# Token sums three chunks later in the attention's first product, a tile of its own for one copy, and another place in memory for the splits of V

## The chip, the core and the metric

The kernel runs on one core of a Trainium2 chip. A core has a matrix engine (TensorE, PE in the profile, with its weight loads as PEld), a vector engine (DVE), a scalar engine (ACT), GpSimd (POOL) and a queue engine (SP); PE writes its results to PSUM, and the other engines move them to the on-chip memory (SBUF). The metric is the device time of one execution in microseconds, as the median of several runs.

## What is computed

A decoder trunk of two residual layers over 512 tokens of 1024 numbers. Layer 0 mixes tokens by causal pooling, layer 1 by dilated window attention with 16 heads; each is followed by a gated feed-forward part (FFN) of width 2816, and one last norm ends the trunk.

```python
def reference(x, ...):
    for i in range(DEPTH):                       # DEPTH = 2
        h = rmsnorm(x, norm_mix[i])
        y = pool_mixer(h, ...) if i % 2 == 0 else attn_mixer(h, ...)
        x = x + y
        h = rmsnorm(x, norm_ffn[i])
        x = x + swiglu(h, ffn_w_gate[i], ffn_w_up[i], ffn_w_down[i])
    return rmsnorm(x, norm_final)

def swiglu(h, w_gate, w_up, w_down):
    return (silu(h @ w_gate) * (h @ w_up)) @ w_down
```

## The kernel before

**Layout and precision.** Everything is transposed: x lies as 8 chunks of 128 features by 512 tokens. A product in full precision is made of three PE products (`mm3`, lines 194 to 196): every operand is split into a rounded part "hi" (a cast on ACT, line 118 for weights, 326 for others) and a rest "lo" (a subtraction on DVE, lines 119 and 327), and hi x hi, hi x lo and lo x hi are added up in PSUM.

**Weights.** One list holds all weight blocks in the order of use. `weights(i)` loads some blocks ahead into `wraw` or `vraw` tiles and splits some ahead into `whi`/`wlo` or `vhi`/`vlo`. There are two kinds, "w" (three split buffers) and "v" (two); "v" blocks exist in the FFN only, where some blocks are sums of two blocks (line 114, and an adding DMA on POOL, line 98).

**FFN.** Pairs of output blocks are made with seven products in the place of eight (`seven`, line 563 is its only matmul, 128x256 each). `quad(n)` makes the gate and up blocks from h; `down(b, half)` multiplies the result u by the down weights. The seven products i = 0 to 6 go to the PSUM tiles p, r, p, q, p, r, p. Products 1, 2 and 5 take a "v" block as weights, the other four a "w" block. A product of a quad has 24 matmuls, one of a down 18. The two layers have 18 quads and 12 such downs in all. The moving operands of a quad are quarters of `h_hi`/`h_lo` (products 0, 1, 3 and 5) and sums of quarters in tiles `t_hi`/`t_lo` (products 2, 4 and 6); those of a down are `u_hi`/`u_lo`.

**What follows a product.** `done(i, ...)` moves each sum out of PSUM. In a quad, product 0 is copied by ACT from p into `ct[:, 0, 0]` (line 581), and product 2 cannot start before that, since it writes p again. `ct` is also what `first_half` and `second_half` of the previous pair read when they split u into `u_hi` (ACT) and `u_lo` (DVE, line 327). So line 581 has to wait until DVE has read the old `ct`:

```python
nc.scalar.copy(ct[:, 0, 0], p)                      # quad, product 0 (line 581)
split(hi[:, 0:2, :], lo[:, 0:2, :], lst[:, 0:2, :])  # the pair before: reads ct[:, 0, 0]
```

A down has three `keep` tiles of its own for such copies (line 620).

**Places in memory.** Pools lie one behind the other in SBUF. Nearly all tiles are multiples of 256 bytes long per partition, and the tiles `h_hi`, `h_lo`, `whi`, `wlo`, `vhi`, `vlo`, `u_hi` and `u_lo` all start 160 bytes past a multiple of 256. `gap4`, a tile of 32 numbers (128 bytes) that nothing uses, moves the six `t` tiles behind it to 32 bytes past a multiple of 256; `gap5`, another such tile, moves what follows back.

**Norm.** The norm factor of a token needs the sum of squares over all features. ACT squares each finished chunk of x (line 246), POOL adds the first six into one tile (line 250), and the last two are kept apart where the FFN of layer 0 ends (`Norm(2)`). `InverseRms.columns` adds up these three tiles per token with 128x1 matmuls (line 269: four token blocks by three tiles), and DVE and ACT make the factor of them (lines 300, 256 to 261) and put it on diagonals (lines 280, 282); `rows` spreads it over the partitions with four matmuls (line 289) and a copy (line 307). The products that need no factor yet go on meanwhile: a hook says before which chunk of a product the two steps stand in PE's order. The first product of the attention (q of heads 0 and 1) begins while the last chunks of x are still being made:

```python
pq = project([j_qk[2 * t]], h_hi, h_lo, KS, None, None if t else {4: inv_rms.columns})
pk = project([j_qk[2 * t + 1]], h_hi, h_lo, KS, None, {2: inv_rms.rows})   # t == 0
```

**Order.** PE's order is the order in which the code is written. On the other engines a scheduler sets the order; each engine then runs its own list strictly in that order.

## Time and profile before

| | |
|---|---|
| runs: median of 3 (lowest to highest) | 1048.31 us (1047.85 to 1048.71) |
| the profiled execution's own time | 1047.12 us |
| its span, first to last instruction | 1045.4 us |
| PE busy | 1018.0 us, 97% of the span |
| DVE busy | 802.6 us, 77% |
| ACT busy | 517.5 us, 50% |
| POOL busy | 189.4 us, 18% |
| mean granted clock of PE | 0.99 of full speed |

Between the profiled execution's time and its span lie 1.7 us. PE is busy nearly all the time, so only three things can change the total: what PE waits for, how fast its matmuls follow each other, and the clock that it is granted. A matmul's duration in the profile overlaps the next one's, so the pace is read from the starts.

### The profile page before, as it was taken

How to read it: one execution, taken by the hardware profiler on the slowest of the kernel's cores; microseconds unless marked ns; L12 is line 12 of the kernel's file. 1: busy time of each engine (PE TensorE's matmuls, PEld its weight loads, DVE VectorE, ACT ScalarE, POOL GpSimd, SP SyncE). 2: the span in 40 equal slices, each digit the busy share in tenths (PEclk: the TensorE clock that was granted, in tenths of full speed). 3: DMA queues.
4: the chain of work that ended last, by engine and by line, in shares of the span. 5: the costliest groups of instructions: out<-in, count | busy, mean ns of one | idle time of the engine just before them, and what ended most of it. 6: DMA issues, size and time to landing. Idle time of an engine off the chain costs nothing.

```text
span 1045.4 us, 17409 instructions
## 1 busy us (share of the span) xinstructions
PE 1018.0 (97%) x6986; PEld 939.5 (90%) x6986; DVE 802.6 (77%) x1100; ACT 517.5 (50%) x797; POOL 189.4 (18%) x163
## 2 busy tenths in 40 slices
PE   8979999999999999999999999999999999999996
PEld 6758888999999999978777899888999999999996
DVE  6794489888888888675988645559989789788844
ACT  6243446554655555452344533454665555455544
POOL 1742300111111111022233210210011110101003
PEclk9989999999999999998999999999999999999998
DMA  7132445669669767432212233524558867966702
GB/s 265 62 101 93 139 120 137 141 175 230 153 162 240 177 137 195 133 113 81 81 41 66 64 114 102 140 81 103 140 140 220 205 148 162 241 157 156 183 35 81
DMA packets 75201, 144.19 MB, mean 138 GB/s; under 512 B 6384, under 2 KB 30576, under 8 KB 75120
## 3 DMA queue, kind: packets, MB, share of 16 engines
q1 hardware_dynamic: 56992, 113.33, 34.5%
q0 software_dynamic: 16320, 28.32, 16.9%
q10 hardware_dynamic: 1808, 1.43, 0.4%
q8 instruction: 54, 0.88, 0.4%
q14 instruction: 27, 0.22, 0.1%
HBM read 140.96 MB, written 2.10 MB: 137 GB/s over the span
## 4 chain that ended last, share of the span: by engine, by line
PE 82%; DVE 10%; issue 3%; DMA 2%; ACT 2%; POOL 1%; SPq 0%; ACTq 0%; DVEq 0%; POOLq 0%
PE p L563 28%; PE r L563 14%; PE mm L194 8%; PE mm L195 8%; PE mm L196 8%; PE mm L563 7%; DVE wlo L119 2%; DMA vraw<-w 1%; PE mm L269 1%; PE mm L1005 1%; PE mm L1004 1%; PE mm L1006 1%; PE early L194 1%; PE tp L871 1%; PE early L195 1%
## 5 line engine op out<-in xcount | busy, mean ns | idle before, releaser
L118 ACT CAST whi<-wraw 128x1024 fp32r<-128x1024 f32 (+4 forms) x201 | 194.2, 967 | 260.8 <-PE p L563 101.8
L119 DVE TENSOR_TENSOR wlo<-wraw,whi 128x1024 fp32r<-128x1024 f32 (+4 forms) x201 | 231.3, 1151 | 40.0 <-ACT whi L118 38.9
L119 DVE TENSOR_TENSOR vlo<-vraw,vhi 128x1024 fp32r<-128x1024 f32 (+1 forms) x90 | 100.3, 1116 | 42.0 <-ACT vhi L118 40.6
L118 ACT CAST vhi<-vraw 128x1024 fp32r<-128x1024 f32 (+1 forms) x90 | 86.8, 965 | 83.6 <-PE r L563 55.6
L196 PE MATMUL mm<-h_hi,wlo 128*128 128x512 f32 x312 | 122.6, 393 | 2.8 <-DVE wlo L119 2.8
L194 PE MATMUL mm<-h_hi,whi 128*128 128x512 f32 x312 | 124.8, 400 | 0.0
L195 PE MATMUL mm<-h_lo,whi 128*128 128x512 f32 x312 | 122.5, 393 | 0.0
L563 PE MATMUL r<-h_hi,vlo 128*128 128x256 f32 x288 | 81.5, 283 | 0.0
L563 PE MATMUL r<-h_lo,vhi 128*128 128x256 f32 x288 | 81.5, 283 | 0.0
L563 PE MATMUL r<-h_hi,vhi 128*128 128x256 f32 x288 | 81.4, 283 | 0.0
L563 PE MATMUL p<-t_hi,whi 128*128 128x256 f32 x288 | 81.2, 282 | 0.0
L563 PE MATMUL p<-t_lo,whi 128*128 128x256 f32 x288 | 81.1, 282 | 0.0
L563 PE MATMUL p<-t_hi,wlo 128*128 128x256 f32 x288 | 81.0, 281 | 0.0
L196 PEld LDWEIGHTS mm<-h_hi,wlo 128*128 128x128 f32 x312 | 59.1, 189 | 16.0 <-DVE wlo L119 3.2
L194 PEld LDWEIGHTS mm<-h_hi,whi 128*128 128x128 f32 x312 | 59.2, 190 | 14.4 <-issue 1.7
L195 PEld LDWEIGHTS mm<-h_lo,whi 128*128 128x128 f32 x312 | 59.2, 190 | 11.8
L114 DVE TENSOR_TENSOR vraw<-vraw,wraw 128x1024 f32<-128x1024 f32 (+1 forms) x60 | 66.7, 1112 | 0.6
L563 PE MATMUL p<-u_hi,whi 128*128 128x256 f32 x216 | 61.2, 283 | 0.1
L563 PE MATMUL p<-u_hi,wlo 128*128 128x256 f32 x216 | 61.1, 283 | 0.0
L563 PE MATMUL p<-u_lo,whi 128*128 128x256 f32 x216 | 61.1, 283 | 0.0
L98 POOL DMA_DIRECT2D wraw<-w x18 | 21.8, 1209 | 216.1 <-DVE ct L513 47.9
L250 POOL TENSOR_TENSOR ssq<-ssq,sq 128x512 f32<-128x512 f32 x20 | 32.2, 1608 | 141.2 <-issue 76.4
(278 smaller groups left out, 3012.7 us busy)
## 6 DMA issues: line engine op xcount, KB each, us to landing
wraw<-w SPq DMA_DIRECT2D x131, 512.0 KB, 3.8
wraw<-w_down SPq DMA_DIRECT2D x48, 384.0 KB, 3.4
vraw<-w SPq DMA_DIRECT2D x18, 512.0 KB, 6.1
vraw<-w POOLq DMA_DIRECT2D x18, 512.0 KB, 7.4
wraw<-w POOLq DMA_DIRECT2D x18, 512.0 KB, 7.4
vraw<-w_down SPq DMA_DIRECT2D x12, 384.0 KB, 4.0
vraw<-w_down POOLq DMA_DIRECT2D x12, 384.0 KB, 5.8
wraw<-w_down POOLq DMA_DIRECT2D x12, 384.0 KB, 7.3
```

Of the source, the lines that this page charges most:

```text
L98: nc.gpsimd.dma_start(dst, more, accum_op=ALU.add)
L114: nc.vector.tensor_add(raw[:, :n], raw[:, :n], raws[item["plus"]][:, :n])
L118: nc.scalar.copy(hi[:, :n], raw[:, :n])
L119: nc.vector.tensor_sub(lo[:, :n], raw[:, :n], hi[:, :n].bitcast(F32))
L194: nc.tensor.matmul(ps, lhsT=whi, rhs=xhi, start=first, stop=False)
L195: nc.tensor.matmul(ps, lhsT=whi, rhs=xlo, start=False, stop=False)
L196: nc.tensor.matmul(ps, lhsT=wlo, rhs=xhi, start=False, stop=last)
L250: nc.gpsimd.tensor_add(self.ssq, self.ssq, sq)
L269: nc.tensor.matmul(cols[:, i : i + 1], lhsT=sq[:, b * P : (b + 1) * P], rhs=ones[:, :1], start=j == 0, stop=j == len(parts) - 1,)
L563: nc.tensor.matmul(ps[:, g, :], lhsT=w[:, g, c, :], rhs=xx, start=i in (0, 1, 3) and g + c + k == 0, stop=c == n - 1 and k == 2, skip_grou ...
L871: nc.tensor.transpose(tp[:, j, :], todo[i + j], ident)
L1004: nc.tensor.matmul(o, lhsT=xh, rhs=whi[:, kk, :], start=kc == 0, stop=False)
```

## The change

It has four edits.

- In the attention's first product the token sums stand before chunk 7 in place of chunk 4, and the spreading of the factor before chunk 4 of the next product in place of chunk 2.
- In a quad, the copy of product 0 goes into `keep[0]`, and the sum after product 3 reads it from there. The three `keep` tiles are made once for the FFN and shared by quads and downs.
- `gap5` moves to a pool of its own between the pool of V and that of the early u tiles. Behind `gap4` without it, `ct`, `keep`, `vraw`, `vhi` and `vlo` now start 32 bytes past a multiple of 256; the u tiles stay where they were.
- Of the `t` tiles the pair for product 2 (the one of a "t" sum with a "v" block) lies ahead of `gap4`, at 160 bytes; the other two pairs lie behind it, at 32 bytes as before.

```diff
@@ ffn
             pools["v"] = open_pool("ffv", 2)
+            open_pool("ffg", 1).tile([P, 32], F32, name="gap5")
             early_u = open_pool("ffa", 2)
...
+            t_tile = lambda i, part: fp.tile([P, 4, 256], F32R, name=f"t_{part}{i}")
+            t2 = [t_tile(2, part) for part in ("hi", "lo")]
             fp.tile([P, 32], F32, name="gap4")
-            T_hi = [block(h_hi, 0, 1)] + [fp.tile([P, 4, 256], F32R, name=f"t_hi{i}") for i in range(1, 4)]
-            T_lo = [block(h_lo, 0, 1)] + [fp.tile([P, 4, 256], F32R, name=f"t_lo{i}") for i in range(1, 4)]
-            fp.tile([P, 32], F32, name="gap5")
+            t3, t4 = ([t_tile(i, part) for part in ("hi", "lo")] for i in (3, 4))
+            T_hi, T_lo = ([block(h, 0, 1), t2[i], t3[i], t4[i]] for i, h in enumerate((h_hi, h_lo)))
...
             lst = ct.rearrange("p m n g c -> p (m n g) c")
+            keep = [fp.tile([P, 2, 256], F32, name=f"keep{i}") for i in range(3)]
@@ quad, done
                     if i == 0:
-                        nc.scalar.copy(ct[:, 0, 0], p)
+                        nc.scalar.copy(keep[0], p)
...
                     elif i == 3:
-                        nc.vector.tensor_add(ct[:, 0, 0], q, ct[:, 0, 0])
+                        nc.vector.tensor_add(ct[:, 0, 0], q, keep[0])
@@ down
-                keep = [fp.tile([P, 2, 256], F32, name=f"keep{i}") for i in range(3)]
@@ attention
-            pq = project([j_qk[2 * t]], h_hi, h_lo, KS, None, None if t else {4: inv_rms.columns})
+            pq = project([j_qk[2 * t]], h_hi, h_lo, KS, None, None if t else {7: inv_rms.columns})
             if t == 0:
-                pk = project([j_qk[2 * t + 1]], h_hi, h_lo, KS, None, {2: inv_rms.rows})
+                pk = project([j_qk[2 * t + 1]], h_hi, h_lo, KS, None, {4: inv_rms.rows})
```

On PE, the rows just ahead of the token sums in the attention's first product. Before, they are those of chunk 3 (the waits in brackets name the engines waited for):

```order
L194 MATMUL mm<-h_hi,whi 128x512 [waits Activation_49]
L195 MATMUL mm<-h_lo,whi 128x512
L196 MATMUL mm<-h_hi,wlo 128x512
L269 MATMUL mm<-ones,ssq 128x1 [waits DVE_49,Pool_49]
L269 MATMUL mm<-ones,sq 128x1 [waits Activation_49] x2
```

In the changed kernel they are those of chunk 6, which waits for its own halves of h:

```order
L194 MATMUL mm<-h_hi,whi 128x512 [waits Activation_49]
L195 MATMUL mm<-h_lo,whi 128x512 [waits DVE_49]
L196 MATMUL mm<-h_hi,wlo 128x512
L269 MATMUL mm<-ones,ssq 128x1 [waits Pool_49]
L269 MATMUL mm<-ones,sq 128x1 [waits Activation_49] x2
```

Nine matmuls, those of chunks 4 to 6, have gone from behind the sums to a place ahead of them; the spreading has six more behind the sums' product ahead of it.

On DVE, what makes the factor of the token sums and the first step of the rotation of q (the shuffle). Before:

```order
L300 TENSOR_SCALAR v_4775<-mm 128x4 [waits PE_49]
L257 RECIPROCAL r_4790<-r_4790 128x4 [waits Activation_49]
L258 TENSOR_TENSOR v_4775<-v_4775,r_4790 128x4 [waits DVE_49]
L282 TENSOR_SCALAR diag<-ident,rB_4795 128x128
L766 STREAM_SHUFFLE ropeb<-mm 128x512 [waits PE_49]
```

In the changed kernel:

```order
L300 TENSOR_SCALAR v_4773<-mm 128x4 [waits PE_49]
L769 STREAM_SHUFFLE ropeb<-mm 128x512 [waits PE_49]
L257 RECIPROCAL r_4788<-r_4788 128x4 [waits Activation_49]
L258 TENSOR_TENSOR v_4773<-v_4773,r_4788 128x4 [waits DVE_49]
L282 TENSOR_SCALAR diag<-ident,rB_4793 128x128
```

The shuffle, which waits for the end of the whole q product, now stands ahead of the factor's small steps.

On ACT, the copy of product 0 of the first quad of a layer. Before:

```order
L326 CAST u_hi<-ct 128x512 [waits DVE_49]
L581 COPY ct<-p 128x512 [waits DVE_49,PE_49]
L326 CAST u_hi<-ct 128x1280 [waits DVE_49]
L118 CAST vhi<-vraw 128x1024 [waits PE_49]
L118 CAST vhi<-vraw 128x1024 [waits DMASW1_49,PE_49]
```

In the changed kernel:

```order
L326 CAST u_hi<-ct 128x512 [waits DVE_49]
L585 COPY keep_1006<-p 128x512 [waits PE_49]
L326 CAST u_hi<-ct 128x1280 [waits DVE_49]
L118 CAST vhi<-vraw 128x1024 [waits PE_49]
L118 CAST vhi<-vraw 128x1024 [waits DMASW1_49,PE_49]
```

The copy keeps its place in ACT's list and no longer waits for DVE.

## Rows read from the trace of the kernel before

**Rows 1.** The page, part 1: each engine's busy time, share, instructions.
```profile
PE 1018.0 (97%) x6986; PEld 939.5 (90%) x6986; DVE 802.6 (77%) x1100; ACT 517.5 (50%) x797; POOL 189.4 (18%) x163
```

**Rows 2.** Waits of PE, whole span: total us, times, longest.
```profile
PE mm L269 <- ACT sq L246: 2.3, 2, 1.8
PE p L563 <- ACT ct L581: 1.9, 2, 1.7
```

**Rows 3.** Timeline of PE: start, us, shapes, count [idle before, releaser]; attention's first product.
```profile
463.89 0.39 PE L194 MATMUL mm<-h_hi,whi 128*128 128x512 f32 x1
...
466.61 0.28 PE L269 MATMUL mm<-ones,ssq 128*128 128x1 f32 x2
467.41 0.38 PE L269 MATMUL mm<-ones,sq 128*128 128x1 f32 x2 [0.52 <-ACT sq L246]
469.55 0.38 PE L269 MATMUL mm<-ones,sq 128*128 128x1 f32 x2 [1.76 <-ACT sq L246]
...
472.67 0.77 PE L194 MATMUL mm<-h_hi,whi 128*128 128x512 f32 x1
...
477.84 0.39 PE L194 MATMUL mm<-h_hi,whi 128*128 128x512 f32 x1
```

**Rows 4.** Timeline of DVE and ACT in the same stretch.
```profile
466.87 0.75 DVE L316 SCALAR_TENSOR_TENSOR h_lo<-x,g_sb,h_hi 128x512 fp32r<-128x512 f32 x1 [0.79 <-ACT h_hi L315]
469.47 0.74 DVE L316 SCALAR_TENSOR_TENSOR h_lo<-x,g_sb,h_hi 128x512 fp32r<-128x512 f32 x1
474.08 0.48 DVE L282 TENSOR_SCALAR diag<-ident,rB 128x128 f32<-128x128 f32 x2
478.05 0.74 DVE L766 STREAM_SHUFFLE ropeb<-mm 128x512 f32<-128x512 f32 x1
...
468.89 0.61 ACT L246 ACTIVATE sq<-x 128x512 f32<-128x512 f32 x1
478.70 0.69 ACT L280 ACTIVATE diag<-ident,rB 128x128 f32<-128x128 f32 x2
```

**Rows 5.** Stretches of PE: us, busy (matmuls), granted clock, DMA share, GB/s.
```profile
466.70:470.80 4.10, 1.82 (x16) 1.00 0.62 215
470.90:477.70 6.80, 6.80 (x22) 0.50 0.19 67
...
68.20:71.50 3.30, 1.54 (x6) 1.00 0.24 97
71.60:78.30 6.70, 4.88 (x11) 0.50 0.50 157
...
124.30:126.00 1.70, 1.70 (x17) 1.00 1.01 376
...
174.40:176.10 1.70, 0.08 (x1) 1.00 0.63 169
```

**Rows 6.** Timeline of PE and ACT at layer 0's first quad.
```profile
176.14 0.39 PE L563 MATMUL p<-t_hi,vhi 128*128 128x256 f32 x1 [1.66 <-ACT ct L581]
...
173.38 0.62 ACT L326 CAST u_hi<-ct 128x512 fp32r<-128x512 f32 x1 [0.77 <-DVE ct L486]
175.50 0.59 ACT L581 COPY ct<-p 128x512 f32<-128x512 f32 x1 [1.50 <-DVE u_lo L327]
```

**Rows 7.** Chain that ended last, by time: start, us, matmuls of one FFN product.
```profile
244.22 2.88 PE r L563 x24
247.10 2.85 PE p L563 x24
...
303.68 2.16 PE r L563 x18
```

**Rows 8.** Costliest groups, shapes apart: count | busy us, mean ns of one | idle.
```profile
L327 DVE TENSOR_TENSOR h_lo<-hn,h_hi 128x1024 fp32r<-128x1024 f32 x6 | 7.3, 1217 | 0.3 <-ACT h_hi L326 0.3
L327 DVE TENSOR_TENSOR t_lo<-t,t_hi 128x1024 fp32r<-128x1024 f32 x6 | 7.3, 1211 | 0.0
```

**Rows 9.** Stretch of a quad's end and a down: PE, PEld, DVE, ACT, POOL busy.
```profile
298.70:314.50 15.80, 15.80 (x134) 15.80 (x134) 15.33 (x22) 9.86 (x15) 1.20 (x1) 1.00 0.63 153
```

## The prediction

> **What bounds the kernel now.** I read the page's busy times first: PE is busy for 1018.0 of 1045.4 us [rows 1], so an edit is worth what it does to PE's waits, to the pace of its matmuls or to its clock, and nothing else. Then the waits of PE over the whole span, longest first: two of them are at places that the diff touches, 2.3 us for squares in the attention's first product and 1.9 us for the copy of product 0 in a quad [rows 2]. Then the timeline around these two, the stretches with their granted clock, and, for the change of places in memory, the chain of waits, whose pieces give the pace of one FFN product after the other.
>
> **Token sums.** Chunks 0 to 3 are twelve matmuls from 463.89 to 466.61, where the sums begin: at full clock 128x512 matmuls start 0.227 us apart. The sums begin at once, but the squares of chunks 6 and 7 aren't there: PE stands 0.52 us and 1.76 us, and the matmul that needs the last square starts at 469.55 [rows 3], right behind ACT's square of 468.89 + 0.61 [rows 4]. That start is set by ACT and stays. In the changed kernel the nine matmuls of chunks 4 to 6 fill the hole: 9 x 0.227 = 2.04 us, from 466.61 to 468.65. Are their operands there? Chunk 6 would begin at 466.61 + 6 x 0.227 = 467.97 and its second matmul, which reads h_lo, at 468.20; DVE has that h_lo at 466.87 + 0.75 = 467.62 [rows 4], so yes, with 0.6 us to spare. The sums that need no last square (about 0.45 us) come after 468.65 and end before 469.55. So the rest of the sums starts when it did, and behind it stand nine matmuls less: **a gain of 2.04 us**, if the clock does what it did.
>
> Chunk 7 stands behind the sums, and its h_lo is ready at 469.47 + 0.74 = 470.2, before they end. The spreading needs the diagonals. DVE's shuffle now stands ahead of the factor's small steps and waits for the end of q, and with it wait ACT's diagonals and PE's four spreading matmuls. With T for the end of the sums: q ends at T + 0.7 at full clock (three matmuls), the shuffle takes 0.74, and from the sums' end at 472.67 to the end of DVE's diagonals took 474.08 + 0.48 - 472.67 = 1.9 us, of which some 1.4 now come behind the shuffle [rows 3, 4]: T + 3.0. ACT's pair, which starts half a microsecond before DVE's end, takes 0.69, and the cast ahead of it waits for q's end as before: 478.70 + 0.69 was 1.55 us behind that end at 477.84, and would be T + 2.3. So the diagonals are there at about T + 3.2. PE reaches the spreading after 3 + 12 matmuls, at T + 3.4. Nothing, or some tenths, is waited for; at half clock PE comes at T + 6.4 and there is room. I take nothing.
>
> **The clock.** This is the term I cannot fix. After the standing and the 128x1 sums, the granted clock is 0.50 (1.2 GHz of 2.4) from 470.9 to 477.7 [rows 5]. What that costs: between 472.67 and 477.84 twelve matmuls take 5.17 us where 12 x 0.227 = 2.72 would do, 2.4 us; and the 22 records of sums from 469.55 to 472.67 take 3.12 us where 16 such records took 1.70 at 124.3 [rows 3, 5], so 0.8 us more than at full clock. Together 3.2 us. With the change, the time without 128x512 matmuls shrinks from 466.61-472.67, 6.1 us, to 468.65-472.0, some 3.3 us, with under half a microsecond of standing in it. Nearest rows on either side: at 124.3 a run of sums of 1.7 us without standing kept 1.00; at 174.4 a stand of 1.7 us kept 1.00; the other low clock, from 71.6, came after 3.3 us of which PE worked for 1.54 [rows 5]. By length 3.3 us is nearer to the case that fell; I take **no gain from the clock**, and keep 3.2 us as the other end.
>
> **The copy of product 0.** At 176.14 PE had stood 1.66 us until ACT's copy was done; the copy starts at 175.50, after 1.50 us of waiting for DVE's split of the old `ct`, while ACT had ended its cast at 173.38 + 0.62 = 174.0 [rows 6]. Without that wait the copy runs from about 174.0 to 174.5, and PE, which was through with product 1 at 176.14 - 1.66 = 174.48, stands about 0.1 us: gain 1.55. The waits by this copy are two in the whole span, 1.9 us together [rows 2], so the other one (the first quad of layer 1) is 0.26, and goes altogether; in the other 16 quads the copy comes in time already. What would be late next? Product 2 reads splits that have long been made, and DVE's list is the same but for one sum that moves ahead of an addition; nothing else waits at these places. **Gain 1.8 us**, between 1.0 and 1.9.
>
> **The places in memory.** This edit removes no instruction. In the chain, a product of 24 matmuls with V blocks and h as operands takes 2.88 us (others of the kind 2.87), while one with t tiles, whose place is 128 bytes off that of its weights, takes 2.85 [rows 7]. Same shapes, same counts: 2.875 - 2.85 = 0.025 us for 24, or 1.0 ns for a matmul. In the change all products with V blocks get that distance: products 1 and 5 of 18 quads (18 x 2 x 24 = 864 matmuls) and products 1, 2 and 5 of 12 downs (12 x 3 x 18 = 648, now 2.16 us for 18 [rows 7], where 18/24 of 2.85 is 2.14). Product 2 of a quad had the distance and keeps it, with its two sides exchanged. Sum: 36 x 0.025 + 36 x 0.0225 = **1.7 us**. The trace has no row of weights moved against h or u; the bounds are this and the opposite sign for product 2 alone (below). I take 1.7, since the rows show distance, and no row shows a fast pair without it.
>
> What the row shows here speaks against a rule of the Trainium skill. "TensorE: Matmul & The Clock Gate", in its section "Step-by-step: what each phase is for", says that PE reads weights and moving operand through two independent ports, so that loading the next weights takes no bandwidth from the running matmul. By that rule a distance between the two would be worth nothing and the sum would be 3.8 us; the 2.85 against 2.88 of rows 7 don't agree with it.
>
> **Sum.** 2.04 + 1.8 + 1.7 = 5.5 us. The profiled execution took 1047.12 us and would take 1041.6. It lay 1.2 us under the median of the runs shown; from the median, 1048.31 - 5.5 = **1042.8**.
>
> **Rivals.**
>
> *The clock stays up.* The nine matmuls shorten the slack stretch enough that the fall at 470.9 doesn't come. For it: 1.7 us of sums without standing, and a stand of 1.7 us, both kept 1.00 [rows 5]. Against it: the stretch is still twice that long. A fall that lasts less than 6.8 us lies between. Time: 1042.8 - 3.2 = 1039.6, or about 1041 where the low stretch is halved.
>
> *The pace hangs on the t tiles' own place, not on the distance.* All fast rows have a moving operand at 32 bytes past a multiple of 256 and all slow ones at 160, so the trace can't tell the two. Then the V products gain nothing, and product 2 of the 18 quads, whose t tiles go to 160, loses 18 x 0.025 = 0.45 us: 1042.8 + 1.7 + 0.45 = 1045.0. The rule of the skill named above would give no gain either, and no loss, 1044.5.
>
> *DVE becomes the bound in the downs; slower than before.* In the stretch from 298.7 to 314.5 DVE is busy for 15.33 of 15.80 us [rows 9], so it has 0.47 us a down to spare. The change puts `keep`, `ct`, `vraw` and the V splits elsewhere, so additions there read two operands of different places. If that made DVE's work there longer, the point from which it costs is 0.47 / 15.33 = 3%; at 8%, 12 downs would cost 12 x (1.23 - 0.47) = 9.1 us, and the total would be 1042.8 + 9.1 = 1051.9. Against it: t_lo, whose operands lie 128 bytes apart, takes 1211 ns, and h_lo, whose lie alike, 1217 [rows 8]. So little that I give it 3 in 100.
>
> *The stand in the first quad isn't gained.* If product 2 or what follows finds another operand late, its 1.8 us go to another wait: 1044.6. I found none, 5 in 100.
>
> **How the numbers follow.** Forecast as summed 0.42; clock up, or low for less time, 0.30; no gain by places 0.20 (with either clock); the stand not gained 0.05; DVE 0.03. The range reaches from the clock's other end to the case without gain by places, and beyond that end by the half microsecond by which the runs before lie apart on either side, and the lower end of the copy's gain: 1039.3 to 1045.9. A measurement of this kernel can tell about 0.2% (2.1 us) from no change. Faster by more than that means under 1046.2: all cases but DVE's and a doubling-up of the bad ones, 0.90; within 0.2%: 0.07; slower: 0.03.
>
> **What the profile after would show.** For the sums: PE's wait for squares at line 269 falls from 2.3 to about 0.5 us, and nine 128x512 matmuls start between the old chunk 3 and the sums; wrong if they wait for h_lo or the spreading waits for diagonals. For the clock: the stretch of 0.50 behind the sums, its length. For the copy: no wait of line 563 for it. For the places: products with V blocks at 2.85 us and 2.14 us, product 2 still 2.85; if these stay at 2.88 and product 2 goes there too, the second rival holds. For DVE: no wait of line 563 for `u_lo` or `vlo` in the downs. The prediction would be wrong by most if the clock fell at a new place.

## The result, and the profile after

The changed kernel took 1037.26 us in the median of six runs (1036.61 to 1042.79), the kernel before 1047.82; the ratio of the means is 0.9915 with an interval of 0.9891 to 0.994. That is faster, as forecast, but by 10.6 us in the medians (8.9 in the means) where 5.5 were forecast, and below the low end of the range (1039.3). The profiled execution took 1036.61 us. The six executions are of two kinds: four took 1036.61 to 1037.48 us at a mean granted clock of 0.993, the profiled one among them, and two took 1040.71 and 1042.79 us at 0.987 and 0.986.

The busy times on the page of the changed kernel, whose span is 1034.8 us:

```profile
PE 1011.8 (98%) x6986; PEld 934.4 (90%) x6986; DVE 802.2 (78%) x1100; ACT 517.8 (50%) x797; POOL 189.5 (18%) x163
```

Against [rows 1] PE is busy for 6.2 us less with the same 6986 matmuls. The two larger terms of the forecast are waits and leave its busy time as it was; only the third, the places with 1.7 us, makes it less. Matmuls at half clock count as busy too. So more than the forecast's share has gone from the matmuls themselves.

The waits of PE in the changed kernel (total us, times, longest), where those of [rows 2] were:

```profile
PE mm L269 <- ACT sq L246: 0.4, 1, 0.4
...
PE early L194 <- ACT h_hi L315: 0.3, 1, 0.3
```

The wait for squares fell from 2.3 to 0.4 us. The wait for the copy of product 0 is no longer on the list. The last row belongs to the kernel's first microseconds, which the change doesn't touch; in the execution before it was 0.8.

The timeline of PE around the sums (start, us, shapes, count, idle time and releaser), against [rows 3]:

```profile
465.20 0.28 PE L269 MATMUL mm<-ones,ssq 128*128 128x1 f32 x2
...
466.11 0.38 PE L269 MATMUL mm<-ones,sq 128*128 128x1 f32 x2 [0.41 <-ACT sq L246]
...
468.36 0.48 PE L194 MATMUL mm<-h_hi,whi 128*128 128x512 f32 x1
...
471.90 1.05 PE L289 MATMUL mm<-diag,ones 128*128 128x128 f32 x8
```

DVE and ACT there, against [rows 4]:

```profile
469.35 0.74 DVE L769 STREAM_SHUFFLE ropeb<-mm 128x512 f32<-128x512 f32 x1
470.77 0.70 ACT L280 ACTIVATE diag<-ident,rB 128x128 f32<-128x128 f32 x2 [0.62 <-DVE rB L261]
470.78 0.48 DVE L282 TENSOR_SCALAR diag<-ident,rB 128x128 f32<-128x128 f32 x2
```

The sums begin right behind chunk 6, PE stands 0.41 us for the last square, and chunk 7 follows at 468.36. The diagonals are ready at 471.47, 3.1 us behind that, and PE gets to them at 471.90, 3.5 us behind it: forecast were 3.2 and 3.4, and no wait. The clock in the same stretch, against [rows 5] (us; busy time and instructions of PE, PEld, DVE, ACT and POOL; granted clock, DMA share, GB/s; so in all rows of stretches below):

```profile
465.20:468.40 3.20, 2.79 (x26) 2.70 (x24) 1.57 (x2) 2.14 (x3) 0.00 (x0) 1.00 0.43 118
468.40:471.90 3.50, 3.50 (x16) 2.87 (x17) 2.57 (x10) 1.95 (x4) 0.00 (x0) 1.00 0.13 54
```

It stays at 1.00 (2.4 GHz). The 0.50 (1.2 GHz) for 6.8 us that stood behind the sums in [rows 5] isn't there. The chain that ended last shows the places (start, us, matmuls of one product): product 1 of a quad, with V, then two products of a down, with V and with W, against [rows 7].

```profile
203.10 2.84 PE r L567 x24
...
300.93 2.13 PE r L567 x18
...
305.21 2.16 PE mm L567 x18
```

Products with V went from 2.88 to 2.84 and from 2.16 to 2.13; those with W and h or u hardly moved. Product 2 of a quad, whose two sides changed places, kept its pace: 118.9 ns from start to start before, 118.65 now.

**The whole difference, matmul by matmul.** Both programs issue the same 6986 matmuls, so the time from one start to the next can be set side by side. The order differs only around the sums, which are taken as one piece. From the first start to the last the changed kernel's profiled execution is 10.5 us shorter:

| where | forecast, us | from the two traces, us |
|---|---|---|
| around the sums | -2.04 | -5.23 |
| stands in the FFN (copy of product 0) | -1.8 | -2.12 |
| pace of FFN matmuls with V | -1.7 | -2.15 |
| pace of FFN matmuls with W | 0 | -0.37 |
| first 500 matmuls (nothing changed there) | 0 | -0.55 |
| all else | 0 | -0.10 |

So every term had the right sign, and one of them is off by 3.2 us. That is the term for the clock, of which the prediction said that it could not fix it, and took nothing.

### The profile page after: what moved, and what is told of

Same layout as the page of the kernel before. It is cut to its first block, busy times and chain, and to the rows that moved or that the text cites. A ratio compares the mean times of both kernels' runs of the same rounds, so it can differ in the third digit from the quotient of the medians.

```text
span 1034.8 us, 17396 instructions
## 1 busy us (share of the span) xinstructions
PE 1011.8 (98%) x6986; PEld 934.4 (90%) x6986; DVE 802.2 (78%) x1100; ACT 517.8 (50%) x797; POOL 189.5 (18%) x163
## 4 chain that ended last, share of the span: by engine, by line
PE 84%; DVE 9%; issue 2%; DMA 2%; POOL 1%; ACT 1%; SPq 0%; ACTq 0%; DVEq 0%; POOLq 0%
PE p L567 29%; PE r L567 15%; PE mm L194 8%; PE mm L195 8%; PE mm L196 8%; PE mm L567 7%; DVE wlo L119 2%; PE mm L269 1%; PE mm L1008 1%; PE mm L1007 1%; PE mm L1009 1%; PE early L194 1%; PE tp L874 1%; PE early L195 1%; PE early L196 1%
## 5 line engine op out<-in xcount | busy, mean ns | idle before, releaser
L196 PE MATMUL mm<-h_hi,wlo 128*128 128x512 f32 x312 | 121.8, 390 | 2.8 <-DVE wlo L119 2.8
```

What stands on the lines that cost most here:

```text
L196: nc.tensor.matmul(ps, lhsT=wlo, rhs=xhi, start=False, stop=last)
```

## Experiments

**One part taken back at a time.** Three kernels are the changed kernel with one of its parts as before. They ran together, beside the kernel before (1046.37 us there) and without the changed kernel, so what a part is worth is read from the traces and not from the medians. First the sums of squares:

```diff
-pq = project([j_qk[2 * t]], h_hi, h_lo, KS, None, None if t else {7: inv_rms.columns})
+pq = project([j_qk[2 * t]], h_hi, h_lo, KS, None, None if t else {4: inv_rms.columns})
...
-pk = project([j_qk[2 * t + 1]], h_hi, h_lo, KS, None, {4: inv_rms.rows})
+pk = project([j_qk[2 * t + 1]], h_hi, h_lo, KS, None, {2: inv_rms.rows})
```

> The changed kernel with the sums of squares back behind chunk 4 and chunk 2. Theory: the edit gave 5.2 us in the traces, 2.0 of standing for squares and 3.2 because the clock no longer falls behind the sums. So here PE stands 2.3 us for squares again, the granted clock is 0.50 for 6.8 us behind the sums, and the time is 1037.3 + 5.2 = 1042.5 us. Rival: the clock stayed up for a reason that has nothing to do with this edit (a difference from one execution to the next, or an edit at another place); then it stays up here too, only the standing comes back, and the time is 1037.3 + 2.0 = 1039.3.

It took 1042.85 us (five runs), 0.9967 of the kernel before (0.9955 to 0.9978). The stretches of PE from the sums on:

```profile
463.90:468.00 4.10, 1.82 (x16) 1.65 (x14) 3.24 (x4) 4.08 (x6) 0.00 (x0) 1.00 0.59 207
468.00:474.80 6.80, 6.80 (x22) 5.83 (x23) 1.31 (x7) 0.28 (x2) 0.00 (x0) 0.50 0.20 71
```

The standing and the low clock are both back, and matched matmul by matmul the stretch is 5.24 us longer than in the changed kernel, as the theory had it. Whether the clock would have stayed up without the edit's help can't be told from one execution; more on this below.

Then the copy of product 0:

```diff
-nc.scalar.copy(keep[0], p)
+nc.scalar.copy(ct[:, 0, 0], p)
...
-nc.vector.tensor_add(ct[:, 0, 0], q, keep[0])
+nc.vector.tensor_add(ct[:, 0, 0], q, ct[:, 0, 0])
```

> The changed kernel with the copy of product 0 back in ct. Theory: PE's stand at the start of product 2 in the first quad of layer 0 (1.7 us) and of layer 1 (0.26 us) comes back, 1037.3 + 1.8 = 1039.1 us. Rival: in the changed kernel the splits that the next products read are late anyway (a wait of 0.25 us for h_lo has appeared at product 5 of the first quad), so only some 1.3 us come back, 1038.6.

It took 1041.04 us, 0.9947 of before (0.9935 to 0.9959). The wait is back in PE's list:

```profile
PE p L567 <- ACT ct L585: 2.0, 2, 1.7
```

The stands in the FFN add up to 1.93 us more than in the changed kernel's trace, so the theory holds to a tenth. The median is higher than 1037.3 + 1.9 would be, and this execution shows one reason, in the stretch behind the sums:

```profile
471.70:475.10 3.40, 3.40 (x10) 2.61 (x9) 2.74 (x8) 1.35 (x3) 0.00 (x0) 0.50 0.00 0
```

The sums stand where the changed kernel has them, and yet the clock is 0.50 for 3.4 us behind them, which costs 1.57 us against the changed kernel's trace. (Its first 500 matmuls, which the edit doesn't touch, took 0.8 us more as well.)

Then the places in memory:

```diff
-open_pool("ffg", 1).tile([P, 32], F32, name="gap5")
...
-t2 = [t_tile(2, part) for part in ("hi", "lo")]
 fp.tile([P, 32], F32, name="gap4")
+t2 = [t_tile(2, part) for part in ("hi", "lo")]
 t3, t4 = ([t_tile(i, part) for part in ("hi", "lo")] for i in (3, 4))
+fp.tile([P, 32], F32, name="gap5")
```

> The changed kernel with the places in memory of before (splits of V at the same offset modulo 256 bytes as h and u, all t tiles 128 bytes off). Theory of distance: matmuls with V blocks against h and u go from 118.5 back to 119.9 ns, 1512 of them, 2.1 us, so 1037.3 + 2.1 = 1039.4 us. Rival: the pace of V's matmuls in the changed kernel comes from something else in it (what DVE and ACT do meanwhile); then they stay at 118.5 and the time at 1037.3.

It took 1042.27 us, 0.9954 of before (0.9942 to 0.9965). V's matmuls are 2.10 us slower than in the changed kernel's trace, W's 0.36, so both the forecast gain and the small one that no term had foreseen belong to this edit. Behind the sums the clock was 0.50 for 3.4 us here too.

**The changed kernel again, and the sums in other forms.** By now two of three traced executions with the new place of the sums had a low clock behind them. Four kernels went to one chip; the first is the changed kernel, unaltered.

> The changed kernel itself once more, beside the two above on one chip, to see how often the clock falls behind the sums. Theory: the gain of 3.2 us there is not certain in each execution; with it 1037 us, with 3.4 us at 0.50 some 1.6 us more, with 6.8 us 3.2 more. Rival: it stays at 1.00 here always, and what was longer in the runs that left one edit out came from what they left out.

It took 1039.84 us in the median, from 1036.48 to 1041.96, 0.993 of before (0.9914 to 0.9947). The profiled execution, around the sums:

```profile
466.40:468.90 2.50, 2.09 (x20) 2.01 (x18) 1.56 (x2) 2.12 (x3) 0.00 (x0) 1.00 0.22 55
468.90:475.70 6.80, 6.80 (x21) 5.64 (x21) 3.06 (x10) 1.95 (x4) 0.00 (x0) 0.50 0.16 63
```

The same program that kept 1.00 in the first trace has 0.50 for 6.8 us here, from 2.5 us behind the start of the sums on. Around the sums this execution is 3.21 us longer than the first one, so against the kernel before the edit gains 5.23 - 3.21 = 2.02 us: the forecast of 2.04, which assumed an unchanged clock. The theory holds, the rival (always 1.00) has fallen. Of the six executions two, 1036.48 and 1037.37 us, have the mean granted clock of the first trace, 0.993; the others lie at 0.988 to 0.992.

Next the sums in one piece, but later, so that PE doesn't stand for the last square:

```diff
-pq = project([j_qk[2 * t]], h_hi, h_lo, KS, None, None if t else {7: inv_rms.columns})
+pq = project([j_qk[2 * t]], h_hi, h_lo, KS, None, None)
...
-pk = project([j_qk[2 * t + 1]], h_hi, h_lo, KS, None, {4: inv_rms.rows})
+pk = project([j_qk[2 * t + 1]], h_hi, h_lo, KS, None, {1: inv_rms.columns, 6: inv_rms.rows})
```

> The changed kernel with the sums four matmul groups later still: in one piece behind chunk 1 of the second product, the spreading behind chunk 6. The stand of 0.4 us for the last square goes, the stretch without 128x512 matmuls is 2.8 us instead of 3.3. Theory of the length: between the changed kernel and the one with halves, with 1.00 behind the sums more often than in the changed kernel; 0.4 us less than the changed kernel where the clock stays up in both. Rival, that the standing alone made the clock fall: with none left it stays at 1.00 in every execution.

It took 1041.27 us, 0.9952 of before (0.994 to 0.9964). The timeline of PE at chunk 7, which now stands ahead of the sums, then the stretches from the sums on:

```profile
467.86 0.50 PE L194 MATMUL mm<-h_hi,whi 128*128 128x512 f32 x1 [0.21 <-ACT h_hi L315]
469.10 0.50 PE L195 MATMUL mm<-h_lo,whi 128*128 128x512 f32 x1 [0.74 <-DVE h_lo L316]
```

```profile
470.30:472.40 2.10, 2.10 (x20) 2.06 (x20) 1.54 (x2) 1.67 (x2) 0.00 (x0) 1.00 0.35 144
472.40:479.30 6.90, 6.90 (x21) 5.64 (x21) 1.31 (x7) 0.90 (x3) 0.00 (x0) 0.51 0.20 76
```

PE is busy all through the first row, and the clock falls all the same: no standing among the sums is needed. But the edit didn't do what it was for. PE comes to chunk 7 before its halves of h are there and stands 0.95 us, until 1.3 us before the sums. So the rival that standing makes the clock fall isn't refuted by this run, and the theory of the length isn't tested by it alone. Around the sums this execution is 4.16 us longer than the changed kernel's first trace, which is more than the 3.21 us of the other trace of that kernel. Then the sums in two halves:

```diff
-... None if t else {7: inv_rms.columns})
+... None if t else {7: lambda: inv_rms.half(0)})
...
-... {4: inv_rms.rows})
+... {1: lambda: inv_rms.half(1), 5: inv_rms.rows})
```

(`half(0)` makes the sums of blocks 0 and 1, `half(1)` those of 2 and 3 and then the factor and the diagonals. Six 128x512 matmuls lie between the halves, those of chunk 7 and of the next product's chunk 0; the expectation below speaks of twelve.)

> The changed kernel with the sums in two halves, two token blocks behind chunk 7 of the first product and two behind chunk 1 of the second, twelve 128x512 matmuls between, the spreading a chunk later. Theory that the length of the stretch without 128x512 matmuls decides over the clock: two stretches of under 2 us instead of one of 3.3 us, so 1.00 behind the sums in every execution, and the stand of 0.4 us for the last square stays at most: 1037 us, and no worse than the best runs of the changed kernel at this place. Rival, that the clock falls there for something else (where the execution stands against something that doesn't follow the kernel): 0.50 for 3.4 us or more again in the profiled execution, 1.6 us more.

It took 1037.57 us in the median of four runs, 1037.03 to 1039.27, 0.9918 of before (0.9905 to 0.9931); the changed kernel on the same chip, 0.993 (0.9914 to 0.9947), isn't told from that.

```profile
465.30:467.10 1.80, 1.40 (x13) 1.28 (x11) 1.60 (x2) 0.88 (x2) 0.00 (x0) 1.00 0.22 85
...
468.60:469.90 1.30, 1.30 (x14) 1.28 (x12) 0.27 (x1) 1.28 (x2) 0.00 (x0) 1.00 0.23 91
469.90:478.00 8.10, 8.10 (x41) 6.87 (x42) 4.83 (x13) 2.89 (x6) 3.48 (x3) 1.00 0.19 65
```

The clock is 1.00 all through (also in the stretch between the halves, left out here), in this trace and in the one other with halves (the last kernel below). Over all traces of this study: sums at the old place, 0.50 for 6.8 us in two of two; in one piece at the new place, 0.50 in four of six (for 6.8 us once, 3.4 us three times); one chunk into the second product, 0.50 in the one; in halves, in none of two. That halves avoid it is not shown: if one execution in three stayed up whatever the form, as in one piece, two would do so by chance one time in nine. And of the four executions of this kernel one, without a trace, took 1039.27 us at a mean granted clock of 0.987 (the others 0.991 to 0.993), so the clock fell somewhere in it. Why it falls in one execution and not in the next stays open.

**The pace by itself.** W moved by 128 bytes as V had been, every moving operand left at 160 modulo 256 bytes:

```diff
+wspl.tile([P, 32], F32, name="gap6", bufs=1)
...
-tmp.tile([P, 40], F32, name="gap2")
+tmp.tile([P, 8], F32, name="gap2")
...
-fp.tile([P, 32], F32, name="gap4")
 t3, t4 = ([t_tile(i, part) for part in ("hi", "lo")] for i in (3, 4))
+fp.tile([P, 32], F32, name="gap4")
```

> The changed kernel with the splits of W 128 bytes off as well (weights at 32, whatever moves against them at 160 modulo 256 bytes, the t tiles too). Theory of distance: the 1725 128x256 matmuls of W against h and u go from 119.7 to 118.5 ns, 2.1 us less, 1037.3 - 2.1 = 1035.2 us; the 128x512 matmuls, which all had their two operands at one offset until now, are 227 ns, and if the same 1.2 ns comes off some 1000 of them, 1.2 us more, 1034.0. Rival: it is V's own place that counts (its neighbours in memory, or the tiles of DVE beside it), not the distance; then nothing changes, 1037.3.

It took 1041.37 us, 0.9953 of before (0.9939 to 0.9968), so it is no faster than the changed kernel, which took 1037.26 and 1039.84 us (below) in its two sets of runs. The costliest group of PE, shapes apart (count, busy us, mean ns of one), of the changed kernel first and then of this one:

```profile
L194 PE MATMUL mm<-h_hi,whi 128*128 128x512 f32 x312 | 123.7, 397 | 0.0
```

```profile
L195 PE MATMUL mm<-h_hi,whi 128*128 128x512 f32 x312 | 125.6, 403 | 0.0
```

In the FFN W's matmuls became 1.87 us shorter (2.1 expected), as the theory of distance had it. But the 128x512 matmuls became slower, 227 to 232 ns from start to start; over the 1537 of them that ran at full clock in both traces that is 7.7 us: the expectation of a gain there had the sign wrong. What helps the narrow shape harms the wide one. To see why, matmuls alone, no other engine at work; offset is the moving operand's place less that of the weights.

```diff
+at = {"d0": (0, 0), "d32": (0, 32), "d64": (0, 64), "d96": (0, 96), "d128": (0, 128), "d192": (0, 192),
+      "s0": (128, 128), "s128": (128, 0)}
...
+nc.tensor.matmul(o, lhsT=whi[:, w], rhs=hi[:, m], ...)
+nc.tensor.matmul(o, lhsT=whi[:, w], rhs=lo[:, m], ...)
+nc.tensor.matmul(o, lhsT=wlo[:, w], rhs=hi[:, m], ...)
```

> Leaves the whole computation out: only matmuls in the pattern of the FFN (hi weights against hi and lo, lo weights against hi), 48 for each offset between weights and moving operand, 256 and 512 columns, no DVE or ACT beside them. PSUM tiles d0 to d192 are named by the offset in bytes; s0 and s128 have the weights moved by 128 and the offset 0 and 128. Theory of distance: with 256 columns d0 and s0 pace at 119.9 ns, d128 and s128 at 118.7; with 512 columns d0 and s0 at 227, d128 and s128 at 232, as in the run with W moved; d64 tells whether a smaller offset gives the one without the other. Rival: the pace depends on where each operand lies by itself (s0 differs from d0, s128 from d128), or on DVE and ACT working beside PE (then all eight are alike).

Each row is the stretch from the first of 48 matmuls to the next 48 (records that reach over its edges are counted too): 256 columns at offset 0, 64 and 192, then s0, then 512 columns at 0 and 64.

```profile
56.13:61.89 5.76, 5.76 (x50) 5.75 (x49) 0.00 (x0) 0.00 (x0) 0.00 (x0) 1.00 0.00 0
...
67.55:73.20 5.65, 5.65 (x50) 5.65 (x49) 0.00 (x0) 0.00 (x0) 0.00 (x0) 1.00 0.00 0
84.65:90.10 5.45, 5.45 (x51) 5.45 (x49) 0.00 (x0) 0.00 (x0) 0.00 (x0) 1.00 0.00 0
90.10:95.86 5.76, 5.76 (x51) 5.76 (x50) 0.00 (x0) 0.00 (x0) 0.00 (x0) 1.00 0.01 3
...
101.56:112.47 10.91, 10.91 (x51) 9.01 (x50) 0.00 (x0) 0.00 (x0) 0.00 (x0) 1.00 0.00 0
123.67:134.67 11.00, 11.00 (x50) 9.01 (x48) 0.00 (x0) 0.00 (x0) 0.00 (x0) 1.00 0.00 0
```

From start to start that is 119.9 ns at 0 and at s0, 118.7 at s128, 117.9 at 64 and 113.6 at 192. With 512 columns it is 227 at 0, 229 at 64 and 233 at the other four. So in this run it is the distance and not the place of either (s0 is d0, s128 is d128), it needs no DVE or ACT, and 128 bytes was not the best choice. The prediction held a rule against its row, that of the Trainium skill, "TensorE: Matmul & The Clock Gate", section "Step-by-step: what each phase is for": PE has two independent read ports, and loading the next weights takes no bandwidth from the running matmul. Read as the prediction read it, that the distance between the two is worth nothing, the rule doesn't hold here: with nothing but PE at work, 48 matmuls of one shape take 5.45 us at one distance and 5.76 at another.

A finer table followed, 25 offsets, one line of the program each:

```diff
+def one(o, w, m, a, z): nc.tensor.matmul(...), nc.tensor.matmul(...), nc.tensor.matmul(...)
...
+run(one, 0, 64, 256, ps[0])
+run(one, 0, 64, S, ps[4])
```

> Leaves the whole computation out: 25 offsets between weights and moving operand, each with 48 matmuls of 256 and 48 of 512 columns, one line of the program for each offset, no DVE or ACT beside them. In the run with eight offsets 256 columns took 119.9 ns at 0, 117.9 at 32 and 64, 119.8 at 96, 118.7 at 128 and 113.6 at 192; 512 columns 227 at 0, 229 at 64, 233 at all others. Theory that the distance modulo 256 bytes decides: 256, 512, 320, 448 and 704 bytes give what 0, 0, 64, 192 and 192 give; weights moved by 64 with the moving operand at 0 gives the 113.6 ns of 192, weights at 128 with 64 too, weights at 32 with 224 as well. Rival, that the place of the moving operand alone counts: weights moved by 64 give 119.9 (d0), and 128 with 64 the 117.9 of 64. Open: whether a distance between 128 and 256 is faster still, and whether one of them is fast with 512 columns too.

Its chain in order of time (start, us, 48 matmuls), 256 columns: offset 64 at line 98, 192 at 122, 320 at 137, 448 at 143, and weights moved by 64 at 152.

```profile
123.10 5.44 PE a L98 x48
...
257.50 5.65 PE a L122 x48
...
341.85 5.66 PE b L137 x48
...
375.39 5.44 PE d L143 x48
...
425.53 5.45 PE c L152 x48
```

Here 64 is fast (113.3 ns) and 192 isn't (117.8), the other way about than in the run before, and 320 and 448 are 117.9 and 113.3, not what 64 and 192 give. So the theory that the distance modulo 256 bytes decides fell as it stood. In both runs every offset that is 64 off a multiple of 128 has one of the same two paces, some 113.5 and 117.8 ns, and something else picks between them. The expectation for the shifted weights was half right: weights moved by 64 give the 113.6 of the run before, which this run has not at 192 but at 448. The tiles of hi and lo lay differently to each other in the two runs; and what ran just before differed too, since here a block of 512 columns stands ahead of each block of 256, and there blocks of 256 followed each other. A version of the kernel below shows both paces at one offset. The next table was made at the kernel's own addresses:

```diff
+rights = ((W, 3072, h_at(0, 0)), (V, 2048, h_at(0, 1)), (W, 3072, t), (V, 2048, t), (W, 3072, u), (V, 2048, u))
...
+for s in range(0, 641, 32): run(one, s)
```

> Leaves the whole computation out: the FFN's patterns of matmuls at the addresses that h, the t tiles and the u tiles have in the changed kernel, against the weights of W and of V moved in steps of 32 bytes from 512 bytes below their place in the changed kernel to 128 above it (there V has its place of before), and the 128x512 pattern of h against W at the same steps; one line of the program for each step. No DVE or ACT beside them. Theory that the place of the weights against the moving operand sets the pace by itself: at V's place of the changed kernel h and u against V take 118.5 ns and 128 bytes above it 119.9; W at its place 119.8 against h and u, and 227 with 512 columns; and some step reaches the 113.3 to 113.6 ns of the two tables before. Rival: the pace differences in the kernel come from DVE and ACT working beside PE; then V's two places are alike here. Open: whether a step serves all the 128x256 patterns, and what it costs the 128x512 pattern (233 against 227 would be 6 ns for each).

The chain again: a is h with W, b h with V, c and d t (at 160 modulo 256) with W and V, e and f u with W and V, g 512 columns of h with W. Line 152 is the place of W and V in the changed kernel, line 148 is 64 bytes below it, line 144 is 128 below it, for V the place of before modulo 256.

```profile
301.33 2.88 PE b L144 x24
...
341.12 2.83 PE a L148 x24
343.95 2.72 PE b L148 x24
...
352.11 2.04 PE e L148 x18
...
356.19 5.49 PE g L148 x24
...
385.65 2.84 PE b L152 x24
...
394.22 2.16 PE e L152 x18
396.38 2.13 PE f L152 x18
398.51 5.46 PE g L152 x24
```

The kernel's own numbers come back with no other engine at work: 2.88 and 2.84 for h with V at the old and the new place, 2.16 and 2.13 for u with W and with V (h with W is 2.87 at line 152). At the kernel's addresses the row repeats every 256 bytes over all 21 steps. And in this table 64 bytes below serves all but h with W, for 1.4 ns on a 128x512 matmul; h with W is the pattern that always comes right behind the 512 columns of the step before.

**A version from these tables.** W 64 bytes below its place, V 64 below (modulo 256), t3 and t4 at 160 too; room for it comes from the order of three small tiles and the sizes of the gaps:

```diff
-stat.tile([P, 8], F32, name="gap0")
+tiny = stat.tile([P, 8], F32, name="gap0")[:, :1]
-stat.tile([P, 8], F32, name="gap1")
+ident = stat.tile([P, P], F32, name="ident")
+ones = stat.tile([P, P], F32, name="ones")
...
-ones = stat.tile([P, P], F32, name="ones")
-tiny = stat.tile([P, 1], F32, name="tiny")
...
-ident = stat.tile([P, P], F32, name="ident")
...
-tmp.tile([P, 40], F32, name="gap2")
+tmp.tile([P, 56], F32, name="gap2")
...
-open_pool("ffg", 1).tile([P, 32], F32, name="gap5")
+open_pool("ffg", 1).tile([P, 48], F32, name="gap5")
...
-fp.tile([P, 32], F32, name="gap4")
 t3, t4 = ([t_tile(i, part) for part in ("hi", "lo")] for i in (3, 4))
+fp.tile([P, 16], F32, name="gap4")
```

> The changed kernel with W's splits 64 bytes and V's splits 192 bytes (mod 256) further on, all moving tiles at 160 modulo 256: each weights block lies 64 bytes from its moving operand, on one side or the other. By the table at the kernel's addresses: h with W 119.7 to 117.8 ns (864 matmuls, 1.6 us), h with V 118.4 to 113.35 (864, 4.4), t with W 118.9 to 113.35 (864, 4.8), t with V (432, 2.2), u with W 119.8 to 113.35 (864, 5.6), u with V 118.5 to 113.35 (648, 3.3): 21.9 us less; the 128x512 matmuls 227.3 to 228.75 (some 900), 1.3 us more. Theory that PE's pace is all that counts: 20.6 us less than the changed kernel's 1037 to 1040, so 1017 to 1020. Rival, that DVE becomes the bound in the downs: there DVE is busy for 15.3 of 15.8 us already, PE's 126 matmuls would take 14.3, and DVE keeps the downs at about 15.4; 12 x 1.1 = 13 us of the gain are lost in part or whole, so 1024 to 1033 with waits of PE for u_lo, vlo or wlo.

It took 1021.51 us (six runs, 1016.0 to 1026.95), 0.9762 of before (0.973 to 0.9795). A product of a down in its chain, with V (the four after it take the same, with W too), and the seven products of this down as one stretch (us, busy times of PE, PEld, DVE, ACT, POOL, granted clock), in the changed kernel first and in this one below:

```profile
300.83 2.04 PE r L565 x18
```

```profile
300.93:315.97 15.04, 15.04 (x128) 15.04 (x128) 14.76 (x21) 8.37 (x12) 2.41 (x2) 1.00 0.69 187
```

```profile
300.83:315.11 14.28, 14.28 (x128) 14.28 (x128) 14.22 (x21) 8.38 (x12) 2.41 (x2) 1.00 0.76 193
```

DVE is busy for 14.22 of 14.28 us and PE doesn't wait: the rival with DVE didn't come to pass, by 0.06 us in this down. Over the kernel the FFN's pace gained 23.6 us against the changed kernel's trace (21.9 by the table), the 128x512 matmuls lost 2.8 (1.3 expected), and 8.0 us were given back by new stands and a stretch of low clock behind one of them.

The sum hides a miss of the table. h with W, which it put at 117.8 ns, took 113.9 in the kernel and gained 4.9 us, not 1.6. And products of one kind, at one offset modulo 256 bytes, have both paces here (chain of this version; r is product 1 of a quad, then product 5, both h with V):

```profile
727.51 2.83 PE r L565 x24
...
738.82 2.72 PE r L565 x24
```

At 117.8 ns run the first five products behind the 128x512 matmuls of the attention, with W and V, h and t alike, and some twenty of 210 in all; the rest run at 113 to 114 ns. The kernel with halves below has the same five. So the offset alone doesn't set the pace, and what ran before seems to have a part in it. Why stays open.

What is late at the new stands is neither PE nor DVE (timeline of ACT, DVE and PE at the start of a quad):

```profile
233.60 1.04 ACT L118 CAST vhi<-vraw 128x1024 fp32r<-128x1024 f32 x1 [3.86 <-DMA vraw<-w]
234.56 0.58 ACT L621 COPY keep<-p 128x512 f32<-128x512 f32 x1
...
235.19 0.38 PE L565 MATMUL p<-u_hi,whi 128*128 128x256 f32 x1 [2.61 <-ACT keep L621]
```

PE stands 2.61 us for the copy that frees its PSUM; that copy is queued on ACT behind a cast that waits 3.86 us for a load. Over the kernel ACT's casts into vhi wait for their loads seven times for 17.6 us, in the changed kernel's first trace twice for 6.6. So the faster PE has come up against the DMA, which both theories missed; a smaller stand of the kind can come without it (0.55 us at 234.42 in the trace with the later sums). With the sums in halves on top of it:

```diff
 # the edits of the version above, and
...
-... None if t else {7: inv_rms.columns})
+... None if t else {7: lambda: inv_rms.half(0)})
...
-... {4: inv_rms.rows})
+... {1: lambda: inv_rms.half(1), 5: inv_rms.rows})
```

> The same with the sums of squares in two halves, as in the run with halves. Theory of the length of the stretch without 128x512 matmuls: no low clock behind the sums in any execution, so 0 to 3 us less than the version above, and less scatter; with the places' whole gain 1016 to 1018. Rival: the clock falls elsewhere in its stead, or DVE takes back the places' gain as above; then the two are alike.

It took 1019.94 us in the median of five runs, 1016.56 to 1021.99, 0.9738 of before (0.9711 to 0.9765). No clock of 0.50 stands behind the sums in its trace. From 1021.51 the step is less than the scatter of either, so that halves help here is not shown; both versions are 16 to 20 us below the changed kernel's two medians, which come from other sets of runs.

## Why the prediction was wrong, step by step

**Token sums, standing: right.** 2.04 us were forecast; 2.02 is what the edit gained in the execution in which the clock did as before. h_lo, diagonals and the shuffle's move came out within 0.1 us.

**The clock: the step that failed.** The prediction put "I take **no gain from the clock**, and keep 3.2 us as the other end", since "By length 3.3 us is nearer to the case that fell", and gave a clock that stays up, or is low for less time, 0.30. In the first trace the clock stayed up, and around the sums 5.23 us came where 2.04 were summed: 3.2 of the 5.0 us by which that trace gained more than the forecast. The step is wrong in kind rather than in size: the term isn't one number of the kernel. The same program gained 3.2 us there in one traced execution and nothing in another. Of the six traces with the sums in one piece at the new place, two have 1.00 throughout, three have 0.50 for 3.4 us (which leaves some 1.6 us of gain) and one has 0.50 for 6.8, so that what the prediction called the rival came five times. The mean clocks of the changed kernel's twelve executions agree: six have the 0.993 of the first trace and took 1036.48 to 1037.48 us, six lie below it and took 1039.2 to 1042.79 (the mean doesn't say where in the kernel the clock was low). A forecast of a median had to weigh the outcomes, and this one chose the one that came once.

On which side the median fell is in part luck: four of the first six executions have the 0.993, two of six in the second set, where the changed kernel was only 6.3 us under the kernel before (1046.15 to 1039.84). That this is near the 5.5 us summed is no confirmation, since it has some gain from the clock in it and more from the places than was summed.

Two readings of the prediction are off beside this. From 469.55 to 472.67 there are 20 records of sums and not 22, which makes its price of the low clock 3.4 us in place of 3.2; the two traces of one program gave 3.21. And it subtracted from the median of three runs, 1048.31, where six gave 1047.82, which is 0.5 us of the distance.

**The copy of product 0: right.** 1.8 us forecast, 2.1 in the stands of the FFN, 1.93 by taking it back alone. In the matched starts 0.25 us of the stand at 176 stayed and 0.3 appeared two products on, and layer 1 gained 0.5 where 0.26 was forecast: 1.8 in all. The other 0.3 went from a stand at 234 of the trace before, which is one of a down and not of this copy.

**The places: the mechanism right, the size too small.** 1.7 us were forecast, 2.15 came with V. The term took the pace of t against V for that of h and u against V; a product of 24 came out at 2.84 instead of 2.85, one of 18 at 2.13 instead of 2.14, over 36 products of each kind. That the pace hangs on the t tiles' own place (chance 0.20) is refuted: V's products with h and u, which don't move, became faster, and so they do with PE alone at work. The 0.37 us that W's matmuls gained were in no term; they went when the places were taken back. They lie in the first matmuls of a product: in the downs, W's product behind one of V takes 2.040 us from its first start to its last before and 2.035 after, by four matmuls of 114.7 to 121.8 ns at its start, and the rest are at 120 in both. So a product of W settles by what ran before it, and that is where V's place comes in.

**The rest.** PE's wait for the first h_hi was 0.5 us shorter in the changed kernel's first trace than in that of before, where nothing is changed. In most of the later traces the clock was 0.50 from about 52 us on, ahead of everything that the change touches, and the first 500 matmuls were 0.7 to 2.0 us longer than in that trace (in the three kernels with W moved, slower 128x512 matmuls are part of it), which a range of half a microsecond on either side did not cover. The stretch in the second trace of the changed kernel (us, busy, granted clock):

```profile
52.40:55.90 3.50, 3.14 (x8) 2.48 (x9) 3.47 (x8) 1.56 (x2) 1.84 (x3) 0.51 0.50 147
```

The range was too narrow by this and by the pace: its low end counted the clock's whole gain but no other term's surplus beside it. By its own words, half a microsecond beyond either case and 0.8 us for the copy, it would have been 1039.1 to 1046.3, and 1037.26 lies outside that too.

**DVE as the bound in the downs** did not come, here nor in the version whose downs are 0.76 us shorter.

## What to carry to other kernels

A low clock behind a soft place in PE's work is a draw, not a cost: look at several executions before pricing it, by their mean clocks where there is no trace, and forecast its outcomes with their shares. Ask of an edit that removes a wait where PE comes to stand next: with the sums two chunks further on PE stood 0.95 us ahead of them, where it had stood 0.41 us for the square. And where PE is the bound for 98% of the span, measure the pace of its matmuls by the offset between weights and moving operand at the kernel's own addresses, for every shape, and then again in the kernel: here it was worth 16 to 20 us of 1037, the wide shape wanted another offset than the narrow one, and for one pattern the table was 4 ns off the kernel, probably by what ran ahead of it there.

## What the runs showed of the hardware that was not expected

At full clock a 128x256 matmul, with weights changed for each, takes from 113.3 to 120.2 ns from start to start by the offset between its operands, and a 128x512 one from 227 to 236. The orders differ: offset 0 is among the slowest for 256 columns (119.9) and the fastest for 512 (227). The offset isn't all: at 64 bytes to either side there are two paces, 113.3 and 117.8 ns, and in the last two kernels products of one kind have now the one and now the other, the slower one behind 128x512 matmuls among other places; what picks between them stays open. And the clock fell behind 2.1 us of 128x1 matmuls among which PE never stood, though it had stood 0.95 us until 1.3 us before them; behind the same piece of program it is low for 6.8 us, 3.4 us or not at all.
